# Column mean of an 8192x8192 matrix: two-row loads throughout, chained adds in six shared buffers, and loads split over two queues

## The chip, the cores and the metric

The kernel runs on one core of a Trainium2 chip. The metric is device time in microseconds (us) for one execution of the whole kernel. Lower is better.

## The reference

The input is one matrix of 8192 x 8192 float32 numbers, 268.4 MB. The output is the mean of each column, 8192 numbers:

```python
def reference(x):            # x: (8192, 8192) float32
    return np.mean(x, axis=0)
```

Each input number is read once and enters one addition, so the work is a stream from HBM through the on-chip memory.

## The kernel before

The 8192 rows are taken in 64 row groups of 128 rows (`G = 64`, called g = 0 to 63), one matrix row for each of the 128 partitions of the on-chip memory. A row group is 4 MB, 32 KB in each partition, and is cut into 16 column blocks of `F = 512`. The first 15 (`NBLK`) go to TensorE one block at a time; the last block is treated as four pieces of 128 columns and is called the edge.

**Buffers.** There are two buffers of two row groups (`pairs`, 64 KB per partition each) and one of a single row group (`singles`), and a separate accumulator `acc` of one row group. Together they take 192 KB per partition, and small result tiles come on top.

**Main loop (L79 to L97 in the listing).** Until the last seven row groups it repeats pair, pair, single. A pair is loaded by one transfer in which every partition receives two neighbouring rows, 64 KB of contiguous memory on both sides (L82). A single is loaded by one transfer of 32 KB per partition (L95). Every load is issued by SyncE, called SP. VectorE, called DVE, then adds each row group into `acc` (helper `add`, L74). The very first pair is added into `acc` without an earlier value (L84). The last pair of the loop has its second row group given to TensorE, except the edge (helper `sums`).

**Last seven row groups (L100 to L125).** These are loaded in pieces: four row groups in halves of 16 KB per partition, two in quarters of 8 KB, and the last one in three quarters, a piece of three blocks and a piece of one block. DVE adds every piece of the first six to `acc`. Of the last row group DVE adds only the first quarter, and TensorE sums the rest straight from the buffer.

**TensorE (helper `mm`, L54).** A matmul of one block with a 128 x 32 matrix that holds 1/8192 sums over the 128 partitions. It adds into one of four PSUM banks (`bank0` to `bank3`, four blocks each, in four groups of 32 output rows) or into `edge`. Four matmuls into the otherwise unused tile `idle` stand between the sums of `acc`.

**Results.** As each bank is finished, ScalarE, called ACT, copies it out of PSUM (L140) and issues its store (L142): four copies and four stores in turn on one engine. DVE copies the edge (L145) and SP stores it (L147).

The order on each engine is the order of the program. Waits are semaphores that a framework adds. One instruction carries one wait, and a second one becomes an instruction of its own ahead of it (EventSemaphore). DVE has 49 of these and SP has 44. DVE's whole program has 128 instructions, SP's 106, ACT's 22, GpSimd's 19 and TensorE's 62, where each matmul counts once.

Of the kernel before, what the change touches and what calls it, by code (L numbers as in the profile page):

```python
# [1 line left out]

# [4 lines left out]


@with_exitstack
def kernel(  # L10
    ctx: ExitStack,
    tc: tile.TileContext,
    x: bass.AP,
    out: bass.AP,
):

    nc = tc.nc
    f32 = mybir.dt.float32
    M, N = x.shape  # L30
    P = nc.NUM_PARTITIONS
    F = 512
    W = F // 4
    NBLK = N // F - 1
    G = M // P
    TAIL = 7

    pairs = ctx.enter_context(tc.tile_pool(name="pairs", bufs=2))
    singles = ctx.enter_context(tc.tile_pool(name="singles", bufs=1))
    sg = ctx.enter_context(tc.tile_pool(name="sg", bufs=1))  # L40
    psp = ctx.enter_context(tc.tile_pool(name="psum", bufs=1, space=bass.MemoryType.PSUM))
    resp = ctx.enter_context(tc.tile_pool(name="res", bufs=1))

    acc = sg.tile([P, N], f32, name="acc")
    ones = sg.tile([P, 32], f32, name="ones")
    warm = sg.tile([P, 32], f32, name="warm")
    nc.gpsimd.memset(ones[:], 1.0 / M)  # L47
    nc.scalar.copy(out=warm[:], in_=ones[:])  # L48
    banks = [psp.tile([P, F], f32, name=f"bank{b}") for b in range(4)]
    edge = psp.tile([P, W], f32, name="edge")  # L50
    idle = psp.tile([P, F], f32, name="idle")

    def mm(dst, q, rhs, first, last):
        tc.keep_in_program_order(nc.tensor.matmul(  # L54
            out=dst[32 * q:32 * q + 32, :],
            lhsT=ones[:],
            rhs=rhs,
            start=first,
            stop=last,
            tile_position=(0, 32 * q),  # L60
            skip_group_check=True,
        ))

    def sums(row, blocks, first, last):
        for i in blocks:
            if i < NBLK:
                mm(banks[i // 4], i % 4, row[:, i * F:(i + 1) * F], first, last)
            else:
                for q in range(4):
                    c = i * F + q * W  # L70
                    mm(edge, q, row[:, c:c + W], first, last)

    def add(row, lo, hi):
        nc.vector.tensor_add(out=acc[:, lo:hi], in0=acc[:, lo:hi], in1=row[:, lo:hi])  # L74

    g = 0
    k = 0
    while g < G - TAIL:
        if k % 3 < 2:  # L79
            t = pairs.tile([P, 2, N], f32, name="pair")  # L80
            src = x[g * P:(g + 2) * P, :].rearrange("(p j) c -> p j c", j=2)
            nc.sync.dma_start(out=t[:], in_=src)  # L82
            if g == 0:
                nc.vector.tensor_add(out=acc[:], in0=t[:, 0, :], in1=t[:, 1, :])  # L84
            else:
                add(t[:, 0, :], 0, N)
                if g + 2 < G - TAIL:
                    add(t[:, 1, :], 0, N)
                else:
                    sums(t[:, 1, :], range(NBLK), True, False)  # L90
                    add(t[:, 1, :], NBLK * F, N)
            g += 2
        else:
            t = singles.tile([P, N], f32, name="single")
            nc.sync.dma_start(out=t[:], in_=x[g * P:(g + 1) * P, :])  # L95
            add(t, 0, N)
            g += 1  # L97
        k += 1

    pair_b = pairs.tile([P, 2, N], f32, name="pair")  # L100
    single = singles.tile([P, N], f32, name="single")
    pair_a = pairs.tile([P, 2, N], f32, name="pair")
    pair_c = pairs.tile([P, 2, N], f32, name="pair")
    halves = [(0, 8), (8, 16)]
    quarters = [(8, 12), (12, 16), (0, 4), (4, 8)]
    rows = [
        (pair_b[:, 0, :], halves),
        (pair_b[:, 1, :], halves),
        (single[:], halves),
        (pair_a[:, 0, :], halves),  # L110
        (pair_a[:, 1, :], quarters),
        (pair_c[:, 0, :], quarters),
    ]
    for row, parts in rows:
        for lo, hi in parts:
            cs = slice(lo * F, hi * F)
            nc.sync.dma_start(out=row[:, cs], in_=x[g * P:(g + 1) * P, cs])
            add(row, lo * F, hi * F)
        g += 1
    row = pair_c[:, 1, :]  # L120
    cuts = [(0, 4), (4, 8), (8, 12), (12, 15), (15, 16)]
    for lo, hi in cuts:
        cs = slice(lo * F, hi * F)
        nc.sync.dma_start(out=row[:, cs], in_=x[g * P:(g + 1) * P, cs])
    sums(acc, range(8, NBLK), False, False)  # L125
    sums(acc, range(NBLK, NBLK + 1), True, False)
    for _ in range(4):
        mm(idle, 0, acc[:, N - F:], True, True)
    sums(acc, range(4, 8), False, False)
    for lo, hi in cuts:  # L130
        if hi <= 4:
            add(row, lo * F, hi * F)
            sums(acc, range(lo, hi), False, True)
        else:
            sums(row, range(lo, hi), False, True)
        if hi <= NBLK:
            for b in range(lo // 4, (hi + 3) // 4):
                n = min(hi - 4 * b, 4)
                r = resp.tile([P, F], f32, name=f"r{b}")
                nc.scalar.copy(out=r[:32 * n, :], in_=banks[b][:32 * n, :])  # L140
                o = out[b * 4 * F:(b * 4 + n) * F].rearrange("(q c) -> q c", q=n)
                nc.scalar.dma_start(out=o, in_=r[0:32 * n:32, :])  # L142
        else:
            r = resp.tile([P, W], f32, name="redge")
            nc.vector.tensor_copy(out=r[:], in_=edge[:])  # L145
            o = out[lo * F:hi * F].rearrange("(q c) -> q c", q=4)
            nc.sync.dma_start(out=o, in_=r[0:P:32, :])  # L147


# [1 line left out]
_INS = ['x']  # L151
_OUTS = [((8192,), 'float32')]


# [23 lines left out]
```

## Time and profile before

| | |
|---|---|
| median of 9 runs | 630.99 us (630.78 to 631.51) |
| the profiled execution's own time | 631.51 us |
| its span in the profile | 629.7 us |
| DVE busy | 533.6 us (85%) |
| TensorE busy | 18.4 us (3%) |
| ScalarE busy | 3.8 us (1%) |
| load queue, share of 16 DMA engines | 99.0% |
| bytes moved, mean rate | 268.50 MB, 426 GB/s |

The profile is one execution. Its span runs from the first to the last instruction; 1.81 us of the device time lie outside it. An engine's busy time is the time in which it works on data, and waiting and issuing transfers do not count. "Share of 16 engines" is the time that packets of a queue took, over the span of all 16 transfer engines. A packet is what one transfer engine moves as one piece; here it is 64 KB for a pair, 32 KB for a single, 16 KB for a half and 8 KB for a quarter. When a transfer engine has moved its share of a load, it sends a packet of 4 bytes to the load's semaphore, so the trace holds 16 such times for every load.

### The profile page before, as it was taken

To read this page: it belongs to the slowest core of one execution; us is meant where nothing else is said; L and a number is where in the kernel's file an instruction comes from. 1 tells how busy PE (TensorE), PEld (TensorE's weight loads), DVE (VectorE), ACT (ScalarE), POOL (GpSimd) and SP (SyncE) were. 2 spreads that over 40 slices of the span, in tenths; PEclk is the share of its full clock that TensorE was granted. 3 is DMA by queue.
4 is the path that set the end of the run, shared out by engine and by line. 5 is a ranking of instruction groups with operands and counts; after the bars stand their busy time and mean duration, and the time that the engine had idled before them with its cause. 6 is when DMAs were issued, how large, how long until landed. Compare 5 with 4: busy or idle time off the path is not lost.

```text
span 629.7 us, 486 instructions
## 1 busy us (share of the span) xinstructions
PE 18.4 (3%) x106; PEld 4.7 (1%) x106; DVE 533.6 (85%) x74; ACT 3.8 (1%) x6; POOL 0.3 (0%) x5
## 2 busy tenths in 40 slices
PE   0000000000000000000000000000000000030017
PEld 0000000000000000000000000000000000000001
DVE  0539889889889889899898898888988988989994
ACT  0000000000000000000000000000000000000001
POOL 0000000000000000000000000000000000000000
PEclk9999999999999999999999999999999999995558
DMA  9999999999999999999999999999999999999996
GB/s 400 408 431 439 454 402 464 400 433 433 466 400 466 400 433 433 466 400 466 400 466 400 466 400 466 404 462 404 462 408 458 408 458 408 458 399 430 424 418 264
DMA packets 7961, 268.50 MB, mean 426 GB/s; under 512 B 899, under 2 KB 903, under 8 KB 1174
## 3 DMA queue, kind: packets, MB, share of 16 engines
q1 hardware_dynamic: 7928, 268.44, 99.0%
q10 hardware_dynamic: 30, 0.03, 0.0%
q8 instruction: 1, 0.02, 0.0%
q14 instruction: 2, 0.02, 0.0%
HBM read 268.44 MB, written 0.03 MB: 426 GB/s over the span
## 4 chain that ended last, share of the span: by engine, by line
DMA 59%; DVE 35%; issue 3%; PE 2%; ACT 0%; ACTq 0%; DVEq 0%
DMA pair<-in_x_dram 59%; DVE acc L74 34%; DVE acc L84 1%; PE bank L54 1%; PE idle L54 1%; ACT r L140 0%; ACTq L142 0%; PE edge L54 0%; DVEq L74 0%
## 5 line engine op out<-in xcount | busy, mean ns | idle before, releaser
L74 DVE TENSOR_TENSOR acc<-acc,pair 128x8192 f32<-128x8192 f32 (+3 forms) x59 | 420.5, 7145 | 64.1 <-DMA pair<-in_x_dram 63.3
L74 DVE TENSOR_TENSOR acc<-acc,single 128x8192 f32<-128x8192 f32 (+1 forms) x13 | 104.4, 8035 | 0.4
L84 DVE TENSOR_TENSOR acc<-pair 128x8192 f32<-128x8192 f32 x1 | 8.7, 8693 | 22.5 <-DMA pair<-in_x_dram 22.5
L54 PE MATMUL bank<-pair,ones 128*32 128x512 f32 x52 | 8.7, 723 | 557.1 <-DMA pair<-in_x_dram 557.1
L54 PE MATMUL bank<-acc,ones 128*32 128x512 f32 x30 | 6.6, 815 | 50.4 <-DVE acc L74 50.4
L54 PEld LDWEIGHTS bank<-pair,ones 128*32 128x32 f32 x52 | 2.1, 129 | 562.3 <-issue 559.7
L140 ACT COPY r<-bank 128x512 f32<-128x512 f32 (+1 forms) x4 | 2.3, 584 | 622.2 <-PE bank L54 621.6
L145 DVE COPY redge<-edge 128x128 f32<-128x128 f32 x1 | 0.3, 292 | 5.6 <-PE bank L54 5.6
L54 PE MATMUL idle<-acc,ones 128*32 128x512 f32 x8 | 4.3, 691 | 0.0
L54 PEld LDWEIGHTS bank<-acc,ones 128*32 128x32 f32 x30 | 1.1, 123 | 54.1 <-DVE acc L74 53.0
L48 ACT ACT_TABLE_LOAD x1 | 1.3, 1283 | 0.7 <-PEq L162 0.7
L54 PE MATMUL edge<-acc,ones 128*32 128x128 f32 x8 | 1.3, 418 | 0.0
L54 PEld LDWEIGHTS idle<-acc,ones 128*32 128x32 f32 x8 | 1.1, 134 | 2.6 <-issue 2.5
L54 PE MATMUL edge<-pair,ones 128*32 128x128 f32 x8 | 0.6, 276 | 0.0
L54 PEld LDWEIGHTS edge<-acc,ones 128*32 128x32 f32 x8 | 0.6, 165 | 1.3 <-issue 1.3
L54 PEld LDWEIGHTS edge<-pair,ones 128*32 128x32 f32 x8 | 0.3, 108 | 0.6 <-DMA pair<-in_x_dram 0.5
L48 ACT COPY warm<-ones 128x32 f32<-128x32 f32 x1 | 0.2, 218 | 0.0
L47 POOL MEMSET ones<- 128x32 f32 x1 | 0.1, 124 | 0.3 <-POOLq L162 0.3
L162 POOL MEMSET const-bfloat16-1.0<- 128x1 bf16 x1 | 0.1, 101 | 0.0
L162 POOL MEMSET const-uint8-127<- 128x1 uint8 x1 | 0.1, 101 | 0.0
L162 POOL MEMSET const-float32-0.0<- 128x1 f32 x1 | 0.1, 98 | 0.2 <-issue 0.2
L162 POOL MEMSET const-float32-1.0<- 128x1 f32 x1 | 0.1, 98 | 0.0
## 6 DMA issues: line engine op xcount, KB each, us to landing
single<-in_x_dram SPq DMA_DIRECT2D x11, 4096.0 KB, 31.9
pair<-in_x_dram SPq DMA_DIRECT2D x6, 2048.0 KB, 25.0
pair<-in_x_dram SPq DMA_DIRECT2D x11, 1024.0 KB, 23.5
single<-in_x_dram SPq DMA_DIRECT2D x2, 2048.0 KB, 27.3
pair<-in_x_dram SPq DMA_DIRECT2D x1, 768.0 KB, 16.8
pair<-in_x_dram SPq DMA_DIRECT2D x23, 30.9
pair<-in_x_dram SPq DMA_DIRECT2D x1, 256.0 KB, 12.4
out_dram<-r ACTq DMA_DIRECT2D x3, 8.0 KB
```

The lines of the kernel that those rows point to most:

```text
L47: nc.gpsimd.memset(ones[:], 1.0 / M)
L48: nc.scalar.copy(out=warm[:], in_=ones[:])
L54: tc.keep_in_program_order(nc.tensor.matmul(out=dst[32 * q:32 * q + 32, :], lhsT=ones[:], rhs=rhs, start=first, stop=last, tile_position=( ...
L74: nc.vector.tensor_add(out=acc[:, lo:hi], in0=acc[:, lo:hi], in1=row[:, lo:hi])
L84: nc.vector.tensor_add(out=acc[:], in0=t[:, 0, :], in1=t[:, 1, :])
L140: nc.scalar.copy(out=r[:32 * n, :], in_=banks[b][:32 * n, :])
L145: nc.vector.tensor_copy(out=r[:], in_=edge[:])
L162: nc = _bacc.Bacc("TRN2", target_bir_lowering=False, num_devices=1)
```

## The change

Six buffers of 32 KB per partition, `bufs`, replace the pairs, the singles and the accumulator. The accumulator is buffer 5.

- **First 12 row groups.** Six two-row loads fill buffers (0,1), (2,3), (4,5), and then the same again. There is no accumulator at this stage. Each pair is added into the next pair by one DVE instruction of 128 x 16384: (2,3) += (0,1), (4,5) += (2,3), (0,1) += (4,5), (2,3) += (0,1), (4,5) += (2,3), and then buffer 5 += buffer 4.
- **Row groups 12 to 55.** There are 22 two-row loads into the five remaining buffers in a ring. Of each, the second row group += the first, and then buffer 5 += the second. Where the two buffers of a pair are not neighbours (buffers 0 and 4), the transfer writes two runs of 32 KB per partition.
- **Row groups 56 to 61** are loaded whole, one at a time. Row group 62 is loaded in halves and row group 63 as one half, one quarter, three blocks and one block.
- **TensorE** takes blocks 0 to 4 of row group 61, blocks 8 to 14 of 62, all of 63, and the accumulator. The four `idle` matmuls are gone: there are 50 matmuls for 53.
- **Queues.** SP issues the loads up to row group 28, except that of row group 2, and ACT issues the others (14 two-row loads and 12 smaller ones).
- **Waits.** Where a DVE add would need two waits (13 adds), GpSimd waits for both and then sets one semaphore that DVE waits for. DVE's program has 68 instructions, SP's 41, ACT's 61, GpSimd's 32 and TensorE's 62.
- **Results.** ACT copies banks 0, 1 and 3, and DVE copies bank 2 and the edge. There are three stores in place of five: banks 0 to 2 together and bank 3 on SP, the edge on ACT.

```diff
-        if k % 3 < 2:
-            t = pairs.tile([P, 2, N], f32, name="pair")
-            src = x[g * P:(g + 2) * P, :].rearrange("(p j) c -> p j c", j=2)
-            nc.sync.dma_start(out=t[:], in_=src)
...
+    def load(dst, src):
+        queue = nc.sync if g < 30 and g != 2 else nc.scalar
+        ins = queue.dma_start(out=dst, in_=src).ins
+        tc.add_to_no_dep_group("loads", ins)
+        return ins
...
+    def add(dst, src, dma=None, own=True):
+
+        ins = nc.vector.tensor_add(out=dst, in0=dst, in1=src).ins
+        dmas = dma if isinstance(dma, list) else [dma] if dma else []
+        if dma and own:
+            nop = tc.keep_in_program_order(nc.gpsimd.nop()).ins
+            for o in dmas + adds[-1:]:
+                tc.add_manual_dep(nop, o.name, sync, reason="GpSimd waits for it")
+            for group in ("loads", "adds"):
+                tc.declare_no_dep(ins, group=group, reason="GpSimd waited for it")
+            tc.add_manual_dep(ins, nop.name, sync, reason="waits for both at once")
+        elif dma:
+            tc.declare_no_dep(ins, group="loads", keep=dmas, reason="long landed")
+            tc.declare_no_dep(ins, group="adds", reason="the load waited for it")
+        tc.add_to_no_dep_group("adds", ins)
+        adds.append(ins)
...
+    while g < CHAIN:
+        u = g % U
+        dmas.append(load_pair(u, u + 1))
+        if g == 2:
+            add(bufs[:, u:u + 2, :], bufs[:, u - 2:u, :], dmas)
+        elif g:
+            v = (u - 2) % U
+            add(bufs[:, u:u + 2, :], bufs[:, v:v + 2, :], dmas[-1])
+        g += 2
+    add(acc, bufs[:, U - 2, :])
...
+    while g < G - 8:
+        dma = load_pair((g - CHAIN) % (U - 1), (g + 1 - CHAIN) % (U - 1))
+        add(buf(g + 1), buf(g), dma, own=False)
+        add(acc, buf(g + 1))
+        g += 2
+    while g < G - 3:
+        add(acc, buf(g), load(buf(g), rows(g)))
+        g += 1
+    r61, r62, r63 = [buf(g + j) for j in range(3)]
+    dma = load(r61, rows(g))
+    add(acc[:, 5 * F:], r61[:, 5 * F:], dma)
...
+    for lo, hi in [(0, 8), (8, 12), (12, 15), (15, 16)]:
+        load(r63[:, lo * F:hi * F], rows(g)[:, lo * F:hi * F])
...
+    plan = [
+        (r61, 0, 5),
+        (acc, 8, 15),
+        (r62, 8, 15),
+        (acc, 0, 8),
+        (acc, 15, 16),
+        (r63, 0, 8),
+        (r63, 8, 12),
+        (r63, 12, 15),
+        (r63, 15, 16),
     ]
...
+    nc.scalar.copy(out=res[:, 0, :], in_=banks[0][:])
+    nc.scalar.copy(out=res[:, 1, :], in_=banks[1][:])
+    nc.vector.tensor_copy(out=res[:, 2, :], in_=banks[2][:])
+    tc.keep_in_program_order(nc.scalar.copy(out=res3[:96, :], in_=banks[3][:96, :]))
+    nc.vector.tensor_copy(out=resedge[:], in_=edge[:])
+    nc.sync.dma_start(
+        out=out[0:12 * F].rearrange("(b q c) -> q b c", b=3, q=4), in_=res[0:P:32, :, :])
+    tc.keep_in_program_order(nc.sync.dma_start(
+        out=out[12 * F:15 * F].rearrange("(q c) -> q c", q=3), in_=res3[0:96:32, :]))
+    tc.keep_in_program_order(nc.scalar.dma_start(
+        out=out[15 * F:].rearrange("(q c) -> q c", q=4), in_=resedge[0:P:32, :]))
```

The names that the prediction uses: "load 6" is the load that begins with row group 6, and r63 is the buffer of the last row group.

## The prediction

> **What bounds the kernel now.** I read the busy times first, then the transfer rows, the waits, and last the end of the span.
>
> ```profile
> PE 18.4 (3%) x106; PEld 4.7 (1%) x106; DVE 533.6 (85%) x74; ACT 3.8 (1%) x6; POOL 0.3 (0%) x5
> ...
> DMA  9999999999999999999999999999999999999996
> ...
> q1 hardware_dynamic: 7928, 268.44, 99.0%
> q10 hardware_dynamic: 30, 0.03, 0.0%
> q8 instruction: 1, 0.02, 0.0%
> q14 instruction: 2, 0.02, 0.0%
> ```
>
> No engine is full, while the load queue fills 99.0% of the 16 transfer engines' span. The packets show no idle transfer engine from 1.9 us until about 623.6 us. So a change here pays only by fewer or cheaper packets, an earlier end of the slowest transfer engine, or a shorter path after the last load. The waits agree:
>
> ```profile
> DVE acc L74 <- DMA pair<-in_x_dram: 63.3, 22, 10.7
> ...
> SPq L82 <- DVE acc L74: 349.8, 20, 17.5
> ```
>
> DVE waits 63.3 us for loads. SP waits longer for DVE to free buffers, but that costs nothing, since another load is always in flight. The groups with shapes kept apart give the prices of adds:
>
> ```profile
> L74 DVE TENSOR_TENSOR acc<-acc,pair 128x8192 f32<-128x8192 f32 x43 | 373.8, 8692 | 64.1 <-DMA pair<-in_x_dram 63.3
> L74 DVE TENSOR_TENSOR acc<-acc,pair 128x4096 f32<-128x4096 f32 x6 | 26.2, 4418 | 0.0
> ```
>
> From 8692 and 4418 ns, an add costs 1.0435 ns per column and 0.144 us fixed; 16384 columns are then 17.24 us. The end, by windows (columns: length, busy time and count for PE, PEld, DVE, ACT and POOL, clock, DMA share, GB/s):
>
> ```profile
> 622.00:623.00 1.00, 1.00 (x9) 0.16 (x8) 0.00 (x0) 0.58 (x1) 0.00 (x0) 1.00 0.97 399
> 623.00:624.00 1.00, 0.79 (x8) 0.00 (x0) 0.00 (x0) 0.15 (x1) 0.00 (x0) 1.00 0.82 307
> 624.00:625.00 1.00, 0.40 (x3) 0.15 (x6) 0.00 (x0) 0.43 (x1) 0.00 (x0) 1.00 0.08 29
> ```
>
> At a share of 0.08 the load is not over: of the last load's 16 completion packets most come by 624.08, two at 624.34 and 624.72. Two transfer engines are late, and the last load counts as landed only with the last. The chain of waits then ends so:
>
> ```profile
> 623.85 0.59 ACT r L140
> ...
> 625.01 0.59 ACT r L140
> ...
> 625.63 0.52 ACTq L142
> 626.15 0.04 issue
> 626.19 0.58 ACT r L140
> ```
>
> ACT copies and issues in turn, so bank 3's copy starts at 626.19, although its matmuls are over by 625.7. Its store issues at 626.80 and lands at 628.68; 1.02 us of closing waits lead to 629.70.
>
> Why are two transfer engines late? The two q14 packets (8 KB, instructions) are at 394.98 and 571.12. Beside the first, a 64 KB packet took 3.08 us for 2.42; beside the second a 16 KB packet took 1.02 for 0.61. Each pair of times delays one transfer engine by about 1.0 and 0.7 us, and every later load lands with a spread of 1.15 us for 0.4 before. Because loads are never short of work, the lag is carried to the end.
>
> [...] The trace issues a load in 0.33 to 0.43 us beside 19 us of transfer, so I give the move of loads to ACT no bandwidth. [...] the fetch takes time of the full transfer engines. [...] matmuls run unbroken from 613.77, and the clock is full from 617.4.
>
> **The change, part by part** (its own time 631.51 = span 629.70 + 1.81 around it; 0.52 above the median of 630.99).
>
> *Packets.* Completion packets give the spacing of loads: a pair 19.35 us, a single 9.70, a half 4.895, a quarter 2.484. Before: 23 pairs 445.05, 11 singles 106.7, 8 halves 39.16, 11 quarters 27.32; 618.23. After: 24 contiguous pairs 464.4; 4 pairs written as two runs each, 16 packets of 32 KB at 1.213 us, 77.6; 6 singles 58.2; 3 halves 14.69; 1 quarter 2.48; 617.37. The last two pieces are the same. **Gain 0.86 us**, all on the path, since the transfer engines are full (0.6 to 1.1).
>
> *Fetches.* At 390.88 DVE starts its 63rd shown instruction, at 570.89 its 95th; SP stands at its 50th and 81st. Which fetches, the trace doesn't say. After, DVE has 68 instructions, SP 41, ACT 61, GpSimd 32: the 571 fetch should go in either case, the 395 fetch goes or comes at DVE's last few instructions. With neither, the last load lands like the ordinary engines (624.05 for 624.73). **Gain 0.68 us** (0 to 0.75). A fetch in the last 10 us would give back about 0.6; I give that one chance in four, **0.15 us** lost. This is why moving waits to GpSimd and loads to ACT may matter.
>
> *First loads.* Loads 0 and 2 now run beside each other on two queues, and load 4 behind them. The first add moves from 22.48 to about 41.9 us. DVE then has 5 x 17.24 + 50 x 8.69 + 11.1 = 531.8 us to do and ends far ahead of the loads. But the buffers are tighter: load n+4 may be issued only when the add that waited for n+2 is over, with one pair then in flight. From the last landing: 0.4 us to the add (41.42 to 41.81 before), 0.1 for GpSimd's hop (its own wait takes the place of DVE's extra one, 0.07), 17.24, 0.03 to issue: 17.77. Of 19.35 there are 1.58 us left. An issue reached its first packet in 1.01 us (0.73 to 1.74), which fits. But first packets took 3.2 us for 2.42, which makes the start worth 1.81 us: 0.23 too late. A late load gives the next one as much lead, so three of loads 6 to 14 pay: 0 to 0.7 us. I take **0.3 us lost**. From load 16 on, a buffer is free after 8.7 us of adds, with over 3 us left. Behind GpSimd's waits stands only its next wait; behind DVE's wait stand its adds, and on those wait SP's loads, priced here.
>
> *Queues.* Load 2 stands on ACT ahead of the table load and `warm` copy, which nothing needs before 600. ACT's last loads issue when row group 58 is added, about 30 us before the end, so its copies wait for nothing. SP has only stores left. No cost.
>
> *Tail.* Counting from T, the last data: row group 60 lands at T-29.0, 61 at -19.3, the halves of 62 at -14.4 and -9.5. Adds: 8.69, 6.02, 4.42 and 0.69 us end by T-8.05. TensorE is busy nearly unbroken from T-13.2 (accumulator, 62, accumulator, 63)[...]; without the `idle` matmuls the last ones cost the same. If it stayed cold, the last eleven would cost about 1.5 us more: rounds of four records follow each other in 0.85 us cold (611.57, 612.42) and 0.43 warm (622.73, 623.18), and four such rounds stand last.
>
> *Stores.* Bank 3's copy no longer waits for bank 2's copy and issue; SP stores it. The edge is now last: PE ends at T+1.14, copy to T+1.51, ACT issue, 1.88 us to landing as before, T+3.4, closing 1.02: T+4.4. Before it was 624.73 to 629.70, 4.97. **Gain 0.57 us** (-0.5 to 0.7).
>
> Sum: -0.86 - 0.68 + 0.15 + 0.3 - 0.57 = -1.66. Its profiled time would be 629.85, and 0.52 less for a median: **629.3 us**.
>
> **The rivals.** *First: only packets and stores pay in part.* A fetch falls into the tail, [...] and a transfer engine still ends 0.7 to 1 us late. For it: DVE still has as many instructions as stood at 395. Against it: none fetched between 3 and 394 us. The gain is then 0.86 + 0.57 - 0.3 - 0.3 = 0.8: 630.2 us, no change. The same holds if the lag is there only in the profiled execution.
>
> *Second, slower: the transfer engines run dry in the first six chained loads.* The place is SP's issue of loads 6, 10 and 14 after a 17.24 us add. It decides once landing, hop, add, issue and first packet exceed 19.35 us; I have 18.8 to 19.6. GpSimd has not waited for a load in this trace, so its hop is unbounded here; if hop and start together cost 1.2 us more, each of three late loads loses about 1.4, 4.2 in all: 4.2 - 0.86 - 0.68 - 0.57 = 2.1 slower, 633.1 us. Against it: a semaphore that GpSimd set at 629.15 released SP at 629.19.
>
> *Third: TensorE stays cold,* 1.5 us later: 630.6 us, no change; its unbroken work speaks against it.
>
> **How the numbers follow.** A measurement here can tell about 0.2%, 1.26 us, from no change. The forecast has 65 in 100, of which 10 end within 0.2% (a gain between 0.7 and 1.26); the first and third rivals together 22, of which 3 are faster; the second 13, of which 3 lose less than 1.26 us. Faster 0.58, same 0.32, slower 0.10. The forecast alone spans 628.4 to 630.3 (all best ends, and the start paying 0.7 with one late engine); to hold 8 in 10 the range goes over the first and third rivals to 631.4.
>
> **What would show it.** Right: a DMA row of nines; no or fewer q14 packets before the tail; completion packets of late loads within 0.5 us; the last load landing near 623.5; no gap in the packets at 60, 99 and 138 us; the edge's copy and store last in the chain. Wrong: a DMA share visibly below 1 between 58 and 145 us (the second rival); a clock of 0.5 in the last 5 us (the third); a last landing at 624.5 (the first).

## The result, and the profile after

The change made the kernel slower: a median of 637.7 us (635.5 to 638.81, 9 runs) against 631.08 us. The ratio is 1.0098, with a 95% interval of 1.009 to 1.0107. The prediction was 629.3 us, in a range of 628.4 to 631.4, so it was wrong in size and in direction. The profiled execution took 635.91 us with a span of 634.0, near the low end of the runs, so the losses measured in it are somewhat smaller than the median's.

The page of the kernel after, its busy times, transfer rows and queues:

```profile
PE 14.6 (2%) x100; PEld 4.3 (1%) x100; DVE 532.3 (84%) x60; ACT 3.3 (1%) x5; POOL 0.3 (0%) x5
...
DMA  9999999999999999999999999999999999999996
...
q10 hardware_dynamic: 4008, 151.00, 55.2%
q1 hardware_dynamic: 2294, 117.47, 43.3%
q8 instruction: 1, 0.02, 0.0%
q14 instruction: 1, 0.01, 0.0%
```

The row of nines looks as before, because each slice is 16 us wide and a gap of one microsecond does not show in it. The two load queues together fill 98.5% of the span for 99.0% before. DVE is no busier than before (532.3 for 533.6). So something was lost between the loads. Where it was lost is seen in the chain of waits of the kernel after (columns: start, length, what):

```profile
0.73 41.39 DMA bufs<-in_x_dram
...
42.22 17.23 DVE bufs L75
59.45 0.02 issue
59.47 23.21 DMA bufs<-in_x_dram
82.68 0.04 POOLq L78
82.72 0.02 issue
82.74 17.24 DVE bufs L75
99.98 0.02 issue
100.00 23.65 DMA bufs<-in_x_dram
123.65 0.04 POOLq L78
123.69 0.02 issue
123.71 17.24 DVE bufs L75
```

In this part load and add alternate on the chain with nothing between them: each load waits for an add, and each add waits for the load before. From the issue of load 6 (59.47) to that of load 10 (100.00) is one round, 40.53 us, and the next is 40.97 us. During one round two pairs pass, and back to back they would need 2 x 19.35 = 38.7 us. A load takes 23.2 to 23.65 us from issue to landing here, 3.9 to 4.3 more than its transfer. The time is lost there, not in the add, which takes 17.23 us for a predicted 17.24. In the kernel before, the same view has one load that starts on idle transfer engines, the first, with 2.4 us over its transfer; a later one is issued while another is under way, and stands behind it:

```profile
0.73 21.72 DMA pair<-in_x_dram
...
88.40 31.04 DMA pair<-in_x_dram
```

The packets tell the same. Load 6 is issued at 59.47. The 16 transfer engines end their last packets of load 4 between 60.37 and 60.95 us and start their first ones of load 6 between 60.61 and 62.27, and those packets take 2.6 to 3.3 us for 2.42. At 61.0 us only six of the 16 engines have a packet, at 100.75 two and at 141.65 three; around 121.25 it is ten. In the kernel before it is never fewer than 14 between 5 and 300 us. By the completion packets load 6 then lands on the fastest engine at 80.37 and on the slowest at 82.41, a spread of 2.04 us where load 4 had 0.59. Measured by the slowest, loads 6, 8, 10 and 12 are late by 2.1, 0.7, 1.6 and 0.7 us against 19.35 us for each, and load 14 has lost 5.04 us since load 4: it lands at 162.74 where 60.95 + 5 x 19.35 = 157.70. The rest of the way costs little: at the hand-over from SP to ACT three loads take 0.54 us more than their 58.05, and the last load lands at 628.69 for 624.72 before. With the gains on packets and fetches that the prediction counted the sum closes: 624.72 - 0.86 - 0.68 + 5.04 + 0.54 = 628.76. Two of these terms are forecasts, so this is a check and no proof.

### The profile page after: what moved, and what is told of

Read it like the earlier page. It is cut to its first block, busy times and chain, and to the rows that moved or that the text cites. A ratio compares the mean times of both kernels' runs of the same rounds, so it can differ in the third digit from the quotient of the medians.

```text
span 634.0 us, 404 instructions
## 1 busy us (share of the span) xinstructions
PE 14.6 (2%) x100; PEld 4.3 (1%) x100; DVE 532.3 (84%) x60; ACT 3.3 (1%) x5; POOL 0.3 (0%) x5
## 4 chain that ended last, share of the span: by engine, by line
DMA 53%; DVE 45%; PE 2%; issue 0%; ACT 0%; POOLq 0%
DMA bufs<-in_x_dram 53%; DVE bufs L75 45%; PE bank L143 2%; ACT res L160 0%; POOLq L78 0%; PE edge L143 0%
## 5 line engine op out<-in xcount | busy, mean ns | idle before, releaser
L75 DVE TENSOR_TENSOR bufs<-bufs 128x8192 f32<-128x8192 f32 (+4 forms) x58 | 531.3, 9169 | 92.8 <-POOLq L78 54.8
L143 PE MATMUL bank<-bufs,ones 128*32 128x512 f32 x84 | 14.4, 738 | 615.2 <-DMA bufs<-in_x_dram 609.7
L143 PEld LDWEIGHTS bank<-bufs,ones 128*32 128x32 f32 x84 | 3.8, 125 | 624.1 <-issue 615.0
```

The lines of the kernel that those rows point to most:

```text
L75: ins = nc.vector.tensor_add(out=dst, in0=dst, in1=src).ins
L143: tc.keep_in_program_order(nc.tensor.matmul(out=dst[32 * q:32 * q + 32, :], lhsT=ones[:], rhs=row[:, c:c + (W if i == NBLK else F)], start ...
```

## The experiments

Theory D: in the chain a load is issued so late that the transfer engines run dry, and each restart costs time. Its rivals: the loads of two queues disturb each other (theory Q), GpSimd's detour makes each add late (theory H), or the loss is made at the end of the kernel.

**The ring from the start: no chain.** Nothing of the chain is left, and load 2 goes to SP, since here load 0's add must come early.

```diff
-        queue = nc.sync if g < 30 and g != 2 else nc.scalar
+        queue = nc.sync if g < 30 else nc.scalar
-    CHAIN = 12
+    CHAIN = 0
...
     while g < G - 8:
-        dma = load_pair((g - CHAIN) % (U - 1), (g + 1 - CHAIN) % (U - 1))
+        dma = load_pair(g % (U - 1), (g + 1) % (U - 1))
+        if g == 0:
+            adds.append(nc.vector.tensor_add(out=acc, in0=buf(0), in1=buf(1)).ins)
...
```

> No chain: the accumulator is filled from row groups 0 and 1, and every later pair goes through the ring of five buffers, as row groups 12 to 55 do in the change; all loads up to row group 28 on SP. If the chained loads running dry are the cause (theory D, 5.0 us of landing time in the profile of the change), the median comes to about 631.5 us and the packets show no gap before 300 us. If the use of two queues is the cause (theory Q), the hand-over at row group 30 is still there and it stays above 635. If the tail is the cause, it stays above 635 too.

Measured: 631.06 us against 631.01 for the kernel before, ratio 1.000 (0.9991 to 1.0008). The whole loss is gone. Its chain of waits:

```profile
31.42 30.04 DMA bufs<-in_x_dram
61.45 0.02 issue
61.48 8.70 DVE bufs L75
70.20 29.95 DMA bufs<-in_x_dram
100.15 0.02 issue
100.17 8.70 DVE bufs L75
```

A load takes 30 us from issue to landing here, more than in the chain, and that is good: it stands in the queue for some 10 us while the load ahead still runs. Two pairs pass in 38.7 us (61.48 to 100.17), which is the transfer time. Between 5 and 300 us at least 15 of the 16 transfer engines always have a packet, and the spread of landings is 0.6 us.

**The chain with short adds.** Three kernels keep the chain, its queues and GpSimd's waits, and only shorten the five adds: to half of the columns, as in the diff, and to 7168 and 7680 columns in the same way. The columns that are left out are missing from the result, so these kernels serve for timing alone.

```diff
-            add(bufs[:, u:u + 2, :], bufs[:, u - 2:u, :], dmas)
+            add(bufs[:, u:u + 2, :N // 2], bufs[:, u - 2:u, :N // 2], dmas)
...
-            add(bufs[:, u:u + 2, :], bufs[:, v:v + 2, :], dmas[-1])
+            add(bufs[:, u:u + 2, :N // 2], bufs[:, v:v + 2, :N // 2], dmas[-1])
```

> The five chained adds take only the first 4096 columns of each row group (the other columns of row groups 0 to 9 are left out of the sum), so each lasts about 8.8 us for 17.2; loads, queues and the GpSimd waits are unchanged. Theory D: the buffers come free 8.5 us earlier, no gap at 60, 100, 121 and 142 us, about 631.5 to 632.5 us. Theory Q and the GpSimd hop (theory H): unchanged, 636 to 638.

> The five chained adds take 7168 of the 8192 columns of each row group (the last 1024 columns of row groups 0 to 9 are left out of the sum), 15.1 us each. Theory D with the measured step (0.6 us from landing to add, the add, 0.03, 2.2 us until the transfer engines are at work again): 17.9 us, below the 19.35 us that the other pair lasts: no gap, 631 to 631.6 us. If the cost follows the length of the add evenly, 635.5.

> The same with 7680 columns (the last 512 columns of row groups 0 to 9 are left out), 16.2 us for each chained add. Theory D: 19.0 us against 19.35, just short of the limit for the slowest transfer engine: 631 to 632.5 us, with small or no gaps. If the cost follows the length of the add evenly, about 636.5.

| chained add | median (kernel before, measured beside it) | ratio, 95% interval | lost from load 4 to load 14 in the profile |
|---|---|---|---|
| 8.69 us | 631.06 (631.01) | 0.9999 (0.9991 to 1.0008) | -0.1 us |
| 15.09 us | 631.5 (631.08) | 1.0008 (0.9999 to 1.0016) | 0.7 us |
| 16.16 us | 633.42 (631.08) | 1.0038 (1.0023 to 1.0052) | 1.9 us |
| 17.23 us (the change) | 637.7 (631.08) | 1.0098 (1.009 to 1.0107) | 5.0 us |

The cost does not follow the length of the add evenly: adds of 15.09 us instead of 8.69 cost 0.4 us in the median, no more than these intervals allow for chance, and the last 2.1 us cost 6.2. That is a limit, as theory D says. The half-length kernel came out a little better than the expected 631.5 to 632.5. The limit lies earlier than my step for the 7680 columns had it, for its median is above the expected 632.5. The chain of that kernel shows why:

```profile
58.34 22.41 DMA bufs<-in_x_dram
...
80.81 16.17 DVE bufs L75
96.98 0.02 issue
97.00 24.12 DMA bufs<-in_x_dram
121.12 0.04 POOLq L78
```

The first round, 58.34 to 97.00, takes 38.66 us and just fits into 38.7. The next load then takes 24.12 us, although most transfer engines have not run dry. They end the packets of the load ahead between 99.08 and 99.71, over 2 us after the issue at 97.00, and most go straight on. But six have a first packet of 2.6 to 3.6 us, one starts only at 100.21, and the slowest lands 2.06 us behind the fastest. So the start costs time even when it comes 2 us ahead. From the issue of load 6 until the last engine ended load 4, 1.5 us were left in the change, 2.5 with 7680 columns and 3.6 with 7168; the five loads lost 5.0, 1.9 and 0.7 us.

**All loads on SP,** with the chain as in the change.

```diff
-        queue = nc.sync if g < 30 and g != 2 else nc.scalar
+        queue = nc.sync
```

> All loads on SP; the chained adds and the GpSimd waits unchanged. Theory Q: loads no longer interleave, 631 to 633 us. Theory D: the gaps of the chain stay; only the hand-over's 0.5 us comes back, and one or two instruction fetches may return with SP's longer program (0.7 us): 636 to 638.5.

Measured: 637.12 us, ratio 1.0096 (1.0079 to 1.0112). The loss stays, and with it the rounds of the chain:

```profile
59.25 23.49 DMA bufs<-in_x_dram
82.74 0.04 POOLq L78
82.78 0.02 issue
82.80 17.24 DVE bufs L75
```

The use of two queues is not the cause. Nor does SP's longer program bring a fetch of instructions on q14 among the loads: one comes at 632.52, beside the stores.

**No GpSimd waits,** so that DVE waits for both itself.

```diff
-        if dma and own:
-            nop = tc.keep_in_program_order(nc.gpsimd.nop()).ins
...
-        elif dma:
...
         tc.add_to_no_dep_group("adds", ins)
```

> GpSimd's waits are gone; DVE waits for load and add itself by an extra instruction. Theory H (the hop costs much of the chain's lead): below 634 us. Theory D: the hop took 0.08 us of 20 in the profile, so 636.5 to 638.5.

Measured: 636.33 us, ratio 1.0089 (1.0071 to 1.0106), far above the 634 of theory H and just under the range of theory D; its interval overlaps that of the change. In its chain, 0.10 us lie between the landing at 82.43 and the add at 82.53; in the change it is 0.06 (82.68 to 82.74). GpSimd's detour costs nothing that can be seen here, and theory H falls.

**What became of the gains: the hand-over between the queues, and ACT's stores.** The ring kernel has no loss and was still not faster than the kernel before. Two kernels looked for the rest: the ring with `queue = nc.sync` for every load, and the same with another order of stores.

```diff
+    tc.keep_in_program_order(nc.scalar.dma_start(
+        out=out[0:8 * F].rearrange("(b q c) -> q b c", b=2, q=4), in_=res[0:P:32, 0:2, :]))
+    res2 = sb.tile([P, F], f32, name="res2")
-    nc.vector.tensor_copy(out=res[:, 2, :], in_=banks[2][:])
+    nc.vector.tensor_copy(out=res2[:], in_=banks[2][:])
...
-        out=out[0:12 * F].rearrange("(b q c) -> q b c", b=3, q=4), in_=res[0:P:32, :, :])
+        out=out[8 * F:12 * F].rearrange("(q c) -> q c", q=4), in_=res2[0:P:32, :])
```

> The ring from row group 0 with every load on SP: the hand-over of loads from SP to ACT at row group 30 is gone. In the profile of the first ring kernel the 16 transfer engines finish a load within 0.6 us before the hand-over and within 1.5 us after it, and the last load waits for the slowest. If the hand-over makes that lag (theory Q, small), the last load lands about 0.9 us earlier and the median is about 630.1 us; if an instruction fetch alone makes it, nothing changes, 631.0.

> As the ring with every load on SP, and ACT stores banks 0 and 1 early, SP bank 2 and then bank 3, ACT the edge. ACT's first store took 1.11 us to issue in the ring kernel and 1.14 before, its later ones 0.5. If the first store on ACT is the slow one, the edge's store ends 0.4 to 0.6 us earlier: about 629.6 us, and faster than the kernel before. If the shape of the edge's store is what is slow, nothing changes against the ring with every load on SP.

Measured: 631.43 us (ratio 1.0006, 0.9998 to 1.0015) and 631.82 us (1.001, 1.0002 to 1.0019); the kernel before, measured beside them, 631.08. Both expectations of a gain failed. In the first the spread of landings is 0.46 us up to 449 us and 1.08 from the load after the instruction fetch at 462.6 on, so the fetch alone makes a lag of 0.6 us, and the last load lands no earlier than with the hand-over (623.90 for 623.82). In the second the edge's store was issued in 0.54 us as expected, but bank 3's copy started only at 625.27. Its chain goes back through ACT's early store, which was issued just before, to bank 1's copy and to TensorE's backlog:

```profile
613.76 7.00 PE bank L135 x39
...
623.50 0.59 ACT res L150
624.09 0.02 issue
624.11 1.12 ACTq L151
625.23 0.04 issue
625.27 0.58 ACT res L155
```

**TensorE's backlog at the end.** Three unused matmuls bridge the 5.7 us in which TensorE waits for the accumulator, in the first ring kernel and in the one with the other stores.

```diff
             left[i] -= 1
+        if row is r61:
+            for _ in range(3):
+                tc.keep_in_program_order(nc.tensor.matmul(
+                    out=idle[0:32, :], lhsT=ones[:], rhs=r61[:, 0:F], start=True, stop=True,
+                    tile_position=(0, 0), skip_group_check=True))
```

> The first ring kernel with three unused matmuls behind the five of row group 61, so that TensorE does not stand idle for 5.7 us before the accumulator is ready. In the ring kernels' profiles its clock rises to full at 616.7 or 618.6 us, in the middle of the backlog, and its last bank is summed 0.3 to 0.7 us after the last load needs it. If that backlog is on the path, 0.3 to 0.5 us faster than the first ring kernel: about 630.6 us. If it is hidden, 631.0.

> The same three unused matmuls in the kernel with all loads on SP and an early store on ACT. There the clock rose at 618.6 us and bank 3's store was the last. If TensorE's backlog is what ate the faster store, 631.8 falls to about 630.4 us; if not, it stays at 631.5 or more.

Measured: 630.58 us (ratio 0.9994, 0.9986 to 1.0002) and 630.88 us (0.9995, 0.9987 to 1.0003), with 631.06 for the kernel before. Against the kernel before measured beside each, the same ring kernels without these matmuls stood at +0.05 and +0.74 us, and with them at -0.48 and -0.18. Only the second difference, 0.92 us, is larger than the intervals allow for chance, and only just; the first, 0.53, is not. The windows of the kernel with the other stores show what happened, first without and then with the unused matmuls (busy time and count for PE, PEld, DVE, ACT, POOL, then the clock, DMA share, GB/s):

```profile
612.00:616.00 4.00, 2.23 (x12) 0.59 (x16) 3.89 (x2) 0.00 (x0) 0.00 (x0) 0.50 1.04 442
616.00:620.00 4.00, 4.00 (x26) 1.00 (x22) 2.93 (x2) 0.00 (x0) 0.00 (x0) 0.68 0.96 403
```

```profile
612.00:616.00 4.00, 1.56 (x16) 0.56 (x19) 3.89 (x2) 0.00 (x0) 0.00 (x0) 1.00 1.05 446
616.00:620.00 4.00, 3.10 (x28) 0.79 (x25) 3.60 (x2) 0.00 (x0) 0.00 (x0) 1.00 0.95 399
```

At half clock TensorE takes 2.23 us for 12 matmul records; at full clock it takes 1.56 us for 16 and has time to spare. The chain that ended last then no longer goes back to the backlog, but to the landing of a load:

```profile
591.53 32.62 DMA bufs<-in_x_dram
624.14 0.04 issue
624.19 1.09 PE bank L136 x6
```

From the last landing to the end of the span it takes 5.8 us without and 5.2 with the unused matmuls. So in the kernel with the other stores the backlog did lie on the path. In the first ring kernel that is not shown: its chain already goes back to a landing at 623.64. These two kernels are the best here, but their intervals still touch 1: neither is shown to beat the kernel before.

**Fewer packets alone, in the kernel before.**

```diff
-    halves = [(0, 8), (8, 16)]
-    quarters = [(8, 12), (12, 16), (0, 4), (4, 8)]
+    halves = [(0, 16)]
+    quarters = [(8, 16), (0, 8)]
```

> The kernel before with one part of the change alone: the four row groups that it loads in halves are loaded whole, and the two in quarters in halves. By the spacing of the loads this saves 4 x (9.79 - 9.70) + 2 x (9.94 - 9.79) = 0.66 us of transfer time. If the packet term of the prediction is right and nothing takes it back, about 630.4 us; if a later DVE or a late transfer engine takes it back, 631.0.

Measured: 635.34 us, ratio 1.0064 (1.005 to 1.0078). That is neither of the two expected times. The last load does land 0.83 us earlier, at 623.89 for 624.72 before. But the kernel ends 10.2 us after it. The chain of its last part:

```profile
612.28 4.43 DVE acc L74
616.71 0.04 issue
616.75 2.15 PE bank L54 x9
...
620.82 3.42 PE idle L54 x7
...
624.67 1.78 PE bank L54 x19
626.45 0.02 issue
626.47 0.59 ACT r L140
```

A coarser piece comes later as a whole, so DVE is behind; TensorE starts its sums 5 us later (616.75 for 611.57 before) and works at half clock until 621.5. The matmuls, and behind them ACT's chain of copies and stores, then run after the loads instead of beside them. The gain was there and was given back several times over.

**Whose fetch it is.** Sixteen tiny instructions on DVE at the start of the ring kernel.

```diff
+    tiny = sb.tile([P, 1], f32, name="tiny")
+    for _ in range(16):
+        nc.vector.memset(tiny[:], 0.0)
```

> The first ring kernel with 16 tiny DVE instructions at the start. If the instruction fetch inside the stream (462 us there, with DVE at its 47th instruction) is DVE's, it comes 16 DVE instructions earlier, near 307 us, and a second may appear; if it is another engine's, it stays near 462 us.

The fetch came at 314.5 us, for 462.4 without them, and DVE had 47 instructions behind it in both. It is DVE's. (This kernel ran once, 632.04 us, too little for a comparison of times.)

## Why the prediction was wrong, point by point

**First loads: the step that failed.** It gave the chain 0.3 us of loss and a worst case of 0.7. It was 5.0 us in the profile and 6.6 us in the median, by the kernel with half-length adds (631.06), which differs from the change in nothing but the length of its five adds. The mechanism was stated: issue after a 17.24 us add, one pair in flight, 19.35 us to beat. One term of the sum was mis-sized, the start: 1.81 us from issue to working transfer engines, read from the very first load. That counted the first of the 16 engines to start, 1.01 us after the issue; the last started after 1.65. There all engines start within 0.64 us and the slowest ends 0.5 us after the fastest. In the chain they run dry one after the other while the next load is being set up, start up to 1.7 us apart, and end 2.0 to 2.5 us apart. From issue to landing a load needs 3.9 to 4.3 us over its transfer, where I had 1.81 and 0.4. The other terms were right: landing to add 0.3 to 0.4 for 0.5 (0.6 at the first add), add 17.23 for 17.24, issue 0.02 for 0.03. So was the time that they leave for the start, 1.5 us for 1.58; the start needs more than twice that.

The second mistake in that step was to let a late load give its successor "as much lead", so that only three of five pay. That holds for an engine, not for a load: the chain waits for the slowest engine of each load, and all of loads 6, 8, 10 and 12 were late. The alternation is there, with 2.1, 0.7, 1.6 and 0.7 us, but the smaller losses are not nothing.

**The second rival was what happened.** It had the right places, for the engines ran dry after the issues of loads 6, 10 and 14, and the right limit, with 13 chances in 100. Its price of 4.2 us for three late loads was close to the 5.0 measured over load 14, in part by luck: it put the surplus on GpSimd's hop and the start together, at 1.2 us; the hop cost nothing, and the start from issue to landing 1.7 to 2.1 us more than assumed. I preferred the low end of an unknown term that multiplies with every round. Of the signs that were named, the row of nines spoke for the forecast and was of no use, since it can't show gaps of a microsecond.

**Packets: right, as far as single profiles show.** Predicted 0.86 us. The kernel before with coarser pieces lands its last load 0.83 us earlier for a predicted 0.66, with both fetches still in the stream, and the first two ring kernels land at 623.82 and 623.90 for 624.72. It did not become time, because the other parts took it back.

**Fetches: the place right, the gain not had.** After the change no q14 packet stands among the loads: the one in the span comes at 631.42, beside the stores, and the one q8 packet of instructions starts at 628.69, when the last load has landed. That it would go or move to DVE's last instructions was right. But the lag that it left behind (0.6 us in the ring with all loads on SP) was replaced by that of the chain and the hand-over, 1.0 us up to 280 us and 1.5 from 337 us on. So the predicted 0.68 us is in the sum of landings above, but larger losses cover it. What the fetch at 631.42 cost is told under the stores.

**Queues: no bandwidth, as said.** Loads 0 and 2, one on each queue, both end at 41.6 us by their completion packets; in the kernel before, the first two loads come from one queue and end at 41.42. In the change, loads 28 and 30 share the transfer engines at the hand-over. Load 28 lands at 305.7, late, but load 30 lands in time at 317.8. The cost that I put at nothing was a lag: from load 26 to load 32 the spread grows from 0.96 to 1.50 us in the change and from 0.62 to 1.51 in the first ring kernel. In the three kernels with short adds the same hand-over leaves it as it was, within 0.06 us. Why it differs is open.

**Tail: wrong in timing, right in sum.** I let row group 60 be added when it lands. In fact DVE's adds follow each other without a pause from 551 us on, 8.8 us each, so its last piece for TensorE was ready at T-4.6 and not T-8.05. TensorE still finished at 629.83, T+1.14 as predicted with T = 628.69: its edge matmuls started at 629.33, right behind the last landing. The clock rose at 622.24, T-6.45: rounds of weight loads follow each other in 0.86 us before it (619.65, 620.51) and in 0.43 after (622.66, 623.09). So the third rival did not come true. But the margin is thin: in the kernel with the other stores the same backlog was worth 0.9 us.

**Stores: not gained.** Predicted 0.57 us. From the last landing to the end of the span it took 5.3 us after the change, 4.85 in the ring kernel and 5.0 before. In the change the edge's landing was last, 2.70 us after the start of its issue where I had 1.88:

```profile
SPq L193 <- DMA out_dram<-res: 1.2, 1, 1.2
...
SPq L193 <- DMA out_dram<-resedge: 0.6, 1, 0.6
```

ACT took 1.11 us to issue it, not the 0.74 of the store that I had taken the price from, but that is not the reason: in the ring kernel the issue took as long, and the edge landed 1.69 us after its start, before bank 3. What differs is the fetch at 631.42, beside the edge's packets: three of its four completion packets came by 631.54, the fourth at 631.99. The chain with all loads on SP has such a fetch at 632.52, and there too the edge is last, after 2.64 us. So the fetch that I gave one chance in four, at 0.6 us, came and kept the end waiting 0.7 us longer than bank 3. In the ring kernel bank 3's store ate most of the gain instead: it landed 3.57 us after the last load and the closing waits took 1.28, where I had the edge at 3.4 and 1.02.

**What stays open.** The ring kernel's profile ends 1.0 us before that of the kernel before, yet the medians are equal: the two profiled executions stand at opposite ends of their runs, 630.56 us for a median of 631.06 and 631.51 for 630.99. The ring kernel's runs have spans of 628.5 to 628.8 and of 629.2 to 629.4 us, and what makes the two groups was not tried. A candidate, not shown, is the transfer engine on which DVE's fetch falls: in the first ring kernel's profile the fetch left the spread at 1.4 us, and in the profile of the same ring with unused matmuls (631.85 us, the slowest of its 13 runs) it raised it from 1.6 to 2.55. Nor was it settled why transfer engines restart so far apart.

## What to carry to other kernels

When a buffer is freed by the last step of a round, write the round down as wait plus work plus issue and compare it with what the other buffers keep in flight. What is left is the time for the next load's start. In this case 3.6 us left lost 0.7 us over five loads, 2.5 lost 1.9, and 1.5 lost 5.0. The price of a start was set here by the slowest transfer engine: from issue to landing 3.9 to 4.3 us over the transfer in the chain, and 2.4 for the first load of the kernel before. So read it from a load that is issued just as the one ahead of it ends, not from the kernel's first transfer. And when transfers are made coarser or fewer, check what starts later because of them: here the last load landed 0.83 us earlier, and the kernel ended 4.3 us later because DVE and TensorE came later to the last pieces.

## What was not expected of the hardware

In the kernel with all loads on SP, transfer engines that had come apart stayed apart: a spread of 2.4 us from the chain was still 2.4 us 450 us later, and in that trace at least 15 of the 16 engines always have a packet from 165 to 619 us, so none could catch up. In the change, where only three of the 16 have a packet at 141.65 us, the spread fell from 2.37 us at load 12 to 0.99 at load 14. An 8 KB instruction fetch widened the spread in a lasting way too: from 0.46 to 1.08 us in the ring with all loads on SP, by 1.0 us in another ring kernel, and not at all in the first. The first store that ACT issued took 1.08 to 1.14 us wherever it stood in the program, even where ACT had issued 26 loads before. Its second took 0.51 to 0.54.
